# Hybrid decoder layer on one core: convolution ends in the input projection, its layer norm goes through memory in the first merge branch, operands are split in twos, PSUM is reused by bank

## Chip, cores and metric

The kernel runs on one core of one Trainium2 chip. The metric is the device time of one execution in microseconds. TensorE (PE) multiplies, with weights loaded beside it (PEld); VectorE (DVE) and ScalarE (ACT) work element by element; GpSimd (POOL) and SyncE (SP) here mostly issue DMAs. SBUF is the working memory of 128 partitions, PSUM holds matmul results in eight banks.

## The reference, cut to what matters

One layer of width 1024 on 1024 tokens, followed by an RMS norm. All is float32.

```python
h = rms_norm(x, norm_g); z = h @ w_in              # 11 blocks of 1024 columns
u = gelu(z_u); v = layer_norm(gelu(z_v))
br_a = gmlp_spatial_gate(u, v, w_s, b_s) * silu(z_ga)        # mixes tokens within chunks of 128
glu = z_ba * sigmoid(z_bb)
c = causal_depthwise_conv(glu, conv_w, conv_b)               # 31 taps along the tokens
br_b = silu(layer_norm(c, conv_ln_g, conv_ln_b)) * silu(z_gb)
br_c = cross_attention(z_q, mem_n, w_kv) * silu(z_gc)        # 4 heads, 256 memory tokens
merged = sum(sigmoid(z_m[n]) * (br[n] @ w_branch[n]) for n in (a, b, c))
out = rms_norm(x + merged @ w_out, final_norm_g)
```

## The kernel before, in words

Every float32 operand is split into a high half in the 32-bit matmul type and a low half (`split`, lines 73 to 75: ACT casts, DVE subtracts), and a product is three matmuls: high by high, high by low, low by high. Results lie with channels on partitions and tokens along the free axis.

The stages, in order of time:

1. 0 to 55 us: keys and values of the memory tokens are projected and stored (lines 195 to 369).
2. 55 to 155: block V of the input projection, its gelu and norm (lines 384 to 439); token norms, and the sums of input blocks that stage 3 needs.
3. 155 to 922: the other ten blocks of the input projection, in 40 *pairs*. `pair` (456) computes 256 output channels for all tokens from two raw weight tiles `r0`, `r1` with seven products of half size instead of eight, a scheme of sums: `s1 = a21 + a22`, `s2 = s1 − a11`, `s3 = a11 − a21`, `s4 = a12 − s2`, and ready-made input combinations T1 to T4. A product (`prod`, 444) is 12 matmuls of 128x512. The results x, z, y are PSUM banks, put together in `ca`, `cb`; the last two products of a pair and its consumer (`fin1`, `fin2`) are done during the next pair. There are four blocks of ten pairs (696 to 731), one per two tiles of 128 channels: convolution gate BB, convolution value BA, U, gate GA, GC, GB, Q, and three merge gates. GA's consumer `ugate` does the token mixing: 32 more matmuls (line 630) and DVE work.
   Beside it runs the convolution: `conv` (546) is a generator of 31 steps for one tile of 128 channels, the first on ACT, 30 on DVE (line 553). BA's consumer puts two generators in a list; `pump` advances the list by the quota `PUMP[i]` of pair i, spread over seven `fill` calls; the last two pairs have a quota of 2. A finished tile is stored in memory (`cdram`) and added into `csum` by a DMA. The sums of weights for later (`wsums`) advance by `spump`.
4. 922 to 1065: branch a is projected and gated by `merge(0, d)`, d = 0 to 7 (768 to 789, matmuls on line 778, gate on 788), the steps of attention between (`events`, 866). After each d, eight more convolution steps.
5. 1065 to 1153: branch c, `merge(2, d)`. In it the layer norm of the convolution: mean by a matmul with ones, `center` (916: subtract, square, add up), `conv_rstd`, `normed` (920: scale, silu, multiply by the gate). The eight tiles stay in SBUF as `cm`.
6. 1153 to 1306: branch b and the output projection, again with seven products each (`oprod`, 974); then the residual, the last norm, and the stores.

The program lists the work in Python order; the library that builds it arranges each engine's instructions by that order and by when they are ready, and an engine executes them one after another. Loads go by SP's queue, stores and some loads (keys, values, `cm`, `sgb`) by POOL's. A buffer is a slot of a pool: 39 slots of 4 KB per partition for most tiles, 6 for operands (`op`), 4 for half sums (`sum`), 4 for evacuated halves (`half`), 3 for raw weights. PSUM is one pool of 8 single banks up to line 759, then one of 4 double banks (line 760).

Of the kernel before, what the change touches and what calls it, by code (L numbers as in the profile page):

```python
# [39 lines left out]
def trunk(ctx, tc, xt, x, memt, wf, wv, wkf, wkv, mem, wbr, wb1, wo, wst, bs, cols, fng, out):  # L40
# [23 lines left out]
    def half(s="u"):  # L64
        return wpool.tile([P, H], F32, tag="half", name=nm(s), bufs=NHALF)
# [21 lines left out]
    def wchunk(src, raw=None):  # L87
        hi, lo = op((P, 1024), "whi"), op((P, 1024), "wlo")
        split(raw_load(src) if raw is None else raw, hi, lo)
        return hi, lo  # L90
# [48 lines left out]

    def sumsq(src, acc_tile, first, w):  # L140
        if first:
            A.activation(out=acc_tile, in_=src, func=AF.Square)
        else:
            sq = slot(shape=(P, w), s="sq")
            A.activation(out=sq, in_=src, func=AF.Square)
            V.tensor_tensor(acc_tile, acc_tile, sq, ALU.add)
# [112 lines left out]
    for g in range(2):  # L259
        pst = [bank() for _ in range(4)]  # L260
        for j in range(4):
            i = 4 * g + j
            if i == 0:
                hi, lo = op((P, 1024), "whi"), op((P, 1024), "wlo")
# [4 lines left out]
            elif g:  # L269
                hi, lo = wchunk(None, kraw[i])  # L270
            else:
                hi, lo = op((P, 1024), "whi"), op((P, 1024), "wlo")
# [171 lines left out]
    def prod(ps, w, m, start, stop):  # L444
        for k in range(4):
            ks = slice(k * P, (k + 1) * P)
            for j, (a, b) in enumerate(((0, 0), (0, 1), (1, 0))):
                T.matmul(ps, w[:, a, ks], m[k][:, b, :], start=(start and k == 0 and j == 0),  # L448
                         stop=(stop and k == 3 and j == 2), skip_group_check=not start)

    def operand(src):
        o = op()
        split(src, o[:, 0, :], o[:, 1, :])
        return o

    def pair(blk, p, consume, fill=lambda: None, last=False):
        r0, r1 = raw_load(wf[blk, 2 * p]), raw_load(wf[blk, 2 * p + 1])
        a11, a12, a21, a22 = r0[:, :H], r0[:, H:], r1[:, :H], r1[:, H:]
        s1, s2, s3, s4 = [wpool.tile([P, H], F32, tag="sum", name=nm("sum"), bufs=NSUM) for _ in range(4)]
# [13 lines left out]
        def second():  # L473
            o12 = operand(a12)
# [5 lines left out]
        V.tensor_tensor(s4, a12, s2, ALU.subtract)  # L480
# [5 lines left out]
        os2 = operand(s2)  # L486
# [4 lines left out]
        os1 = operand(s1)  # L491
# [3 lines left out]
        os3 = operand(s3)  # L495
# [7 lines left out]
        o22 = operand(a22)  # L503
        os4 = operand(s4)
# [191 lines left out]
    for p in range(4):  # L696
        for i, (blk, fn, then) in enumerate((
# [10 lines left out]
        )):  # L708
            if p == 3 and i == 8:
                for e in range(NPRE):  # L710
                    bra[e] = load(udram[e], s="bra")
            if i == 2:
                spatial_load(p)
            if i >= SP0:
                spump(1)
            share = iter(range(NFILL))

            def fill():
                k = next(share)
                n = PUMP[i] if 10 * p + i < 38 else 2  # L720
                pump(n * (k + 1) // NFILL - n * k // NFILL)

            if (p, i) == (3, 9):
                for e in range(NPRE):
                    branch_tile(e, bra[e])
            pair(blk, p, kept(fn, then), fill, (p, i) == (3, 9))
            if i == 3:
                for g in range(2 * p, 2 * p + NVA):
                    vas[g] = va_load(g)
            if i >= SP0:  # L730
                spump(SPUMP)
# [28 lines left out]
    psum = ctx.enter_context(tc.tile_pool(name="psum", bufs=4, space=PSUM))  # L760
# [40 lines left out]
    def att_q(n):  # L801
# [3 lines left out]
        qh, ql = slot(F32R, (P, 2, H), "qh"), slot(F32R, (P, 2, H), "ql")  # L805
        for d in range(2):
            qf = wpool.tile([P, H], F32, tag="sum", name=nm("qf"), bufs=NSUM)
# [70 lines left out]
    for e in range(NPRE, KT):  # L878
        branch_tile(e, load(udram[e], s="bra"))
        if e == EQ:  # L880
            att_q(0)
    merged = [None] * KT
# [5 lines left out]
    csr = wchunk(None, csum)  # L888

    def tokmean(v):  # L890
        ps = acc()
        for hf in range(2):
            for j in range(2):
                T.matmul(ps[:, hf, :], onesd, v[j][:, hf * H:(hf + 1) * H], start=(j == 0), stop=(j == 1))
        return ps
# [10 lines left out]
    cm = []  # L906
    csq = crb = crs = None

    def conv_rstd():
        nonlocal crs  # L910
        ps = misc()
        for i in range(TT):
            T.matmul(ps[:, i:i + 1], csq[:, i * P:(i + 1) * P], ones[:, 0:1], start=True, stop=True)
        crs = diagonals(mean_rsqrt(ps[:, :TT], TT, LN_EPS), TT)

    def center(e):
        V.tensor_tensor(cm[e], cm[e], csum, ALU.subtract)
        sumsq(cm[e], csq, e == 0, S)

    def normed(e):  # L920
        V.scalar_tensor_tensor(out=cm[e], in0=cm[e], scalar=c1(COL_CLG, e), in1=crb, op0=ALU.mult, op1=ALU.mult)
        A.activation(out=cm[e], in_=cm[e], func=AF.Silu, bias=c1(COL_CLB, e))
        sg = load(sgbdram[e], s="sgb", eng=G)
        V.tensor_tensor(cm[e], cm[e], sg, ALU.mult)

    for d in range(KT):
        g = merge(2, d, conv_rstd if d == 4 else None, 2)
        V.tensor_tensor(merged[d], merged[d], g, ALU.add)
        if d == 0:
            cm = [load(cdram[e], s="cm", eng=G) for e in range(KT)]  # L930
# [244 lines left out]
NFETCH = 3  # L1175
NSLOT = 39
NRAW = 3
NOP = 6
NSUM = 4
NHALF = 4  # L1180
PUMPA = 8
# [61 lines left out]
```

## Time and profile before

| | us |
|---|---|
| median of 3 runs | 1317.36 (1316.32 to 1318.34) |
| the profiled execution | 1315.63 |
| its span, first to last instruction | 1313.9 |

| engine | busy us | share of the span |
|---|---|---|
| PE | 1301.2 | 99% |
| PEld | 1085.8 | 83% |
| DVE | 1088.4 | 83% |
| ACT | 616.9 | 47% |
| POOL | 115.5 | 9% |

Busy time is the union of an engine's instructions; matmuls overlap, so PE's share says that something was always in flight, not how fast. DMA moved 249.74 MB, 190 GB/s on the mean.

### The profile page before, as it was taken

To read this page: it belongs to the slowest core of one execution; us is meant where nothing else is said; L and a number is where in the kernel's file an instruction comes from. 1 tells how busy PE (TensorE), PEld (TensorE's weight loads), DVE (VectorE), ACT (ScalarE), POOL (GpSimd) and SP (SyncE) were. 2 spreads that over 40 slices of the span, in tenths; PEclk is the share of its full clock that TensorE was granted. 3 is DMA by queue.
4 is the path that set the end of the run, shared out by engine and by line. 5 is a ranking of instruction groups with operands and counts; after the bars stand their busy time and mean duration, and the time that the engine had idled before them with its cause. 6 is when DMAs were issued, how large, how long until landed. Compare 5 with 4: busy or idle time off the path is not lost.

```text
span 1313.9 us, 16329 instructions
## 1 busy us (share of the span) xinstructions
PE 1301.2 (99%) x6010; PEld 1085.8 (83%) x6010; DVE 1088.4 (83%) x1468; ACT 616.9 (47%) x1012; POOL 115.5 (9%) x194
## 2 busy tenths in 40 slices
PE   9999999999999999999999999999999999999997
PEld 8788888888888888888888888888888888888886
DVE  6889669989959989976998996896589478895886
ACT  7667644445344445444444434445544443443245
POOL 0100000211000212001111101001000010000000
PEclk9999999999999999999999999999999999999999
DMA  9944324787425777325778436447553654655933
GB/s 340 411 158 153 136 81 132 223 270 219 139 82 161 216 225 239 130 80 166 231 232 244 129 94 158 170 172 255 194 198 123 207 194 144 224 193 220 406 126 128
DMA packets 82016, 249.74 MB, mean 190 GB/s; under 512 B 8336, under 2 KB 18064, under 8 KB 81936
## 3 DMA queue, kind: packets, MB, share of 16 engines
q1 hardware_dynamic: 55552, 153.44, 33.4%
q0 software_dynamic: 26096, 94.91, 23.2%
q8 instruction: 47, 0.77, 0.2%
q10 hardware_dynamic: 288, 0.35, 0.1%
q14 instruction: 33, 0.27, 0.1%
HBM read 176.84 MB, written 68.16 MB: 186 GB/s over the span
## 4 chain that ended last, share of the span: by engine, by line
PE 92%; DMA 4%; ACT 1%; DVE 1%; issue 1%; SPq 0%; POOL 0%; ACTq 0%; POOLq 0%
PE x L448 33%; PE y L448 17%; PE acc L778 12%; PE acc L979 10%; PE z L448 8%; PE b L402 7%; PE acc L819 2%; PE acc L855 1%; DMA raw<-in_wv 1%; PE sp L630 1%; DMA kvraw<-in_wkv 1%; DMA k<-kd 1%; PE acc L840 0%; ACT y L1124 0%; DMA mtok<-in_mem 0%
## 5 line engine op out<-in xcount | busy, mean ns | idle before, releaser
L448 PE MATMUL x<-T,op 128*128 128x512 f32 x1440 | 347.4, 390 | 0.0
L448 PEld LDWEIGHTS x<-T,op 128*128 128x128 f32 x1440 | 270.0, 188 | 56.3 <-ACT u L489 0.5
L74 ACT CAST op<-sum 128x512 fp32r<-128x512 f32 x160 | 99.4, 622 | 122.2 <-PE z L448 57.8
L553 DVE SCALAR_TENSOR_TENSOR conv<-cb,col,conv 128x994 f32<-128x994 f32 (+14 forms) x120 | 151.9, 1266 | 1.3 <-ACT conv L549 0.5
L75 DVE TENSOR_TENSOR op<-sum,op 128x512 fp32r<-128x512 f32 x160 | 109.6, 685 | 24.8 <-ACT op L74 24.6
L448 PE MATMUL x<-B,op 128*128 128x512 f32 x480 | 115.5, 389 | 0.0
L448 PE MATMUL z<-B,op 128*128 128x512 f32 x480 | 115.3, 389 | 0.0
L448 PE MATMUL y<-T,op 128*128 128x512 f32 x480 | 115.3, 389 | 0.0
L448 PE MATMUL y<-B,op 128*128 128x512 f32 x480 | 115.3, 389 | 0.0
L553 DVE SCALAR_TENSOR_TENSOR conv<-ca,col,conv 128x994 f32<-128x994 f32 (+14 forms) x90 | 113.7, 1264 | 0.4
L74 ACT CAST op<-raw 128x512 fp32r<-128x512 f32 x120 | 74.3, 620 | 73.2 <-PE y L448 71.8
L448 PEld LDWEIGHTS z<-B,op 128*128 128x128 f32 x480 | 90.1, 188 | 18.7
L448 PEld LDWEIGHTS y<-T,op 128*128 128x128 f32 x480 | 90.1, 188 | 18.7
L448 PEld LDWEIGHTS y<-B,op 128*128 128x128 f32 x480 | 90.1, 188 | 18.7
L448 PEld LDWEIGHTS x<-B,op 128*128 128x128 f32 x480 | 90.1, 188 | 18.7
L75 DVE TENSOR_TENSOR op<-raw,op 128x512 fp32r<-128x512 f32 x120 | 82.2, 686 | 24.4 <-ACT op L74 24.1
L778 PE MATMUL acc<-bhi,whi 128*128 128x512 f32 x256 | 79.7, 393 | 0.9 <-DVE ca L511 0.9
L778 PE MATMUL acc<-bhi,wlo 128*128 128x512 f32 x256 | 79.2, 390 | 0.0
L778 PE MATMUL acc<-blo,whi 128*128 128x512 f32 x256 | 79.2, 390 | 0.0
L979 PE MATMUL acc<-q,sw 128*128 128x512 f32 x288 | 65.4, 389 | 0.0
L979 PEld LDWEIGHTS acc<-q,sw 128*128 128x128 f32 x288 | 54.1, 188 | 11.2
L498 ACT COPY u<-x 128x512 f32<-128x512 f32 x40 | 23.6, 589 | 81.6 <-PE x L448 81.6
(267 smaller groups left out, 2162.1 us busy)
## 6 DMA issues: line engine op xcount, KB each, us to landing
raw<-in_wf SPq DMA_DIRECT2D x80, 512.0 KB, 3.6
sw<-sw SPq DMA_DIRECT2D x40, 512.0 KB, 7.8
sw<-wsh POOLq DMA_DIRECT2D x20, 512.0 KB, 4.3
sw<-ws POOLq DMA_DIRECT2D x20, 512.0 KB, 3.9
raw<-in_wv SPq DMA_DIRECT2D x16, 512.0 KB, 4.0
raw<-in_wbr SPq DMA_DIRECT2D x16, 512.0 KB, 5.5
gate<-g SPq DMA_DIRECT2D x16, 512.0 KB, 4.4
ws<-in_wb POOLq DMA_DIRECT2D x14, 512.0 KB, 6.4
```

The source lines that it names most:

```text
L74: A.copy(hi, src)
L75: V.tensor_tensor(lo, src, f(hi), ALU.subtract)
L402: T.matmul(pst[t], q[:, a, ts_], w[:, ws], start=(k == 0 and j == 0), stop=(k == KT - 1 and j == 2))
L448: T.matmul(ps, w[:, a, ks], m[k][:, b, :], start=(start and k == 0 and j == 0), stop=(stop and k == 3 and j == 2), skip_group_check=not start)
L498: A.copy(u3, x)
L553: V.scalar_tensor_tensor(out=a[:, PAD - j:], in0=g[:, :n], scalar=col[:, cw + j:cw + j + 1], in1=a[:, PAD - j:], op0=ALU.mult, op1=ALU.add)
L630: T.matmul(ps[:, t * P:(t + 1) * P], va[:, 4 * hf + t, :], ws[:, i, :], start=True, stop=True)
L778: T.matmul(ps[:, hf, :], w[:, ks], m[k][:, hf * H:(hf + 1) * H], start=(k == 0 and j == 0), stop=(k == KT - 1 and j == 2))
L819: T.matmul(ps[:, i, :], q[a][:, d, i * P:(i + 1) * P], kk[:, b, d, :], start=(d == 0 and j == 0), stop=(d == 1 and j == 2))
L855: T.matmul(ps[:, d, :], vv[:, a, m, d * P:(d + 1) * P], p2[b][:, m, :], start=(m == 0 and j == 0), stop=(m == MT - 1 and j == 2))
L979: T.matmul(ps[t], a[k][i][:, ts_], w[k][n], start=(start and k == 0 and j == 0), stop=(k == 3 and j == 2), skip_group_check=not start)
```

## The change

- `op` makes one tile of twice the size, for a high and a low half of 1024 columns; there are 3 of them for 6. A pair splits `r0` whole (a11, a12), then `s2` and `s1`, which lie side by side, then `r1` whole, in which `s4` has taken the place of `a21`. `s3` is split by itself into a `sum` tile. `sum` tiles are twice as wide, 2 for 4. Weight chunks, final operands and the like use the same tiles.
- The 40 pairs have an explicit order: BB and BA of the second and third block come before the last pair of the block before, those of the fourth before the last two. The quotas `PUMP` rise by one nearly throughout, from 55 to 66 per ten pairs, and hold for the last two pairs too.
- In the first merge branch no convolution steps are planned; after d = 0 what is left is done, after d = 1 the mean, after d = 2 to 4 three centrings each, after 5 the deviation, after 6 two, after 7 three of the scalings. Tiles come from memory and go back: centred ones to `ccdram`, finished ones to `brbdram`. Three scalings follow in branch c, then the quarters of the finished tiles are loaded for the last stage.
- The PSUM pool of the merges gets `reuse_waits="tile"`: a tile waits for what used its own banks, not for the whole pool before.
- Four attention units, not two, are stored in memory and loaded again (`NSPILL`).

```diff
-    def op(shape=(P, 2, H), s="op"):
-        return wpool.tile(list(shape), F32R, tag="op", name=nm(s), bufs=NOP)
+    def op(s="op"):
+        return wpool.tile([P, 2, 2 * H], F32R, tag="op", name=nm(s), bufs=NOP)
+    def wide(dt=F32, s="sum"):
+        return wpool.tile([P, 2 * H], dt, tag="sum", name=nm(s), bufs=NSUM)
...
-    def operand(src):
+    def operands(src):
         o = op()
         split(src, o[:, 0, :], o[:, 1, :])
-        return o
+        return [(o[:, 0, v], o[:, 1, v]) for v in (slice(0, H), slice(H, 2 * H))]
 
     def pair(blk, p, consume, fill=lambda: None, last=False):
...
+        s12, s3 = wide(), half("s3")
+        s2, s1 = halves(s12)
         V.tensor_tensor(s1, a21, a22, ALU.add)
         V.tensor_tensor(s2, s1, a11, ALU.subtract)
-        o11 = operand(a11)
+        o11, o12 = operands(r0)
...
         V.tensor_tensor(s3, a11, a21, ALU.subtract)
-        V.tensor_tensor(s4, a12, s2, ALU.subtract)
+        V.tensor_tensor(a21, a12, s2, ALU.subtract)
...
-        os2 = operand(s2)
+        os2, os1 = operands(s12)
...
-        os3 = operand(s3)
+        os3 = halves(wide(F32R, "os3"))
+        split(s3, *os3)
...
-        o22 = operand(a22)
-        os4 = operand(s4)
+        os4, o22 = operands(r1)
...
+    pairs = [(p, i) for p in range(4) for i in range(10)]
+    for p, back in ((1, 1), (2, 1), (3, 2)):
+        at = pairs.index((p, 0))
+        pairs[at - back:at + 2] = [(p, 0), (p, 1)] + pairs[at - back:at]
+    for p, i in pairs:
...
-                n = PUMP[i] if 10 * p + i < 38 else 2
+            n = PUMP[i]
...
-    psum = ctx.enter_context(tc.tile_pool(name="psum", bufs=4, space=PSUM))
+    psum = ctx.enter_context(tc.tile_pool(name="psum", bufs=4, space=PSUM, reuse_waits="tile"))
...
+    def center(e):
+        t = cst.pop(e)
+        center_load(e + 2)
+        V.tensor_tensor(t, t, csum, ALU.subtract)
+        store(ccdram[e], t)
+        if e == 0:
+            cst["q"] = slot(s="csq")
+        sumsq(t, cst["q"], e == 0, S)
...
+    def normed_load(e):
+        if e < KT:
+            cst[e] = load(ccdram[e], s="cn", eng=G), load(sgbdram[e], s="sgb", eng=G)
+    def normed(e):
+        t, sg = cst.pop(e)
+        normed_load(e + 2)
+        V.scalar_tensor_tensor(out=t, in0=t, scalar=c1(COL_CLG, e), in1=cst["r"], op0=ALU.mult, op1=ALU.mult)
+        A.activation(out=t, in_=t, func=AF.Silu, bias=c1(COL_CLB, e))
+        V.tensor_tensor(t, t, sg, ALU.mult)
+        store(brbdram[e], t)
     for d in range(KT):
         merged[d] = merge(0, d, lambda: events(2 * d))
         events(2 * d + 1)
-        pump(PUMPA)
-    pump(10 ** 6)
+        if d == 0:
+            pump(10 ** 6)
+        elif d == 1:
+            conv_mean()
+            center_load(0)
+            center_load(1)
+        elif d < 5:
+            for e in range(3 * d - 6, min(3 * d - 3, KT)):
+                center(e)
+        elif d == 5:
+            conv_rstd()
+            normed_load(0)
+            normed_load(1)
+        elif d == 6:
+            conv_spread()
+            for e in range(2):
+                normed(e)
+        else:
+            for e in range(2, 5):
+                normed(e)
...
+    def quadrant(src, r, c):
+        o = []
+        for j in range(2):
+            t = slot(shape=(P, 2, H), s="quad")
+            for i in range(2):
+                nc.sync.dma_start(out=t[:, i, :], in_=src[4 * r + 2 * j + i][:, c * H:(c + 1) * H])
+                o.append(t[:, i, :])
+        return o
     for d in range(KT):
-        g = merge(2, d, conv_rstd if d == 4 else None, 2)
+        g = merge(2, d, None)
         V.tensor_tensor(merged[d], merged[d], g, ALU.add)
...
+        if d < 3:
+            normed(5 + d)
+        elif d in (4, 5):
+            quads[d - 4, 0] = quadrant(brbdram, d - 4, 0)
+        elif d > 5:
+            quads[d - 6, 1] = quadrant(brbdram, d - 6, 1)
...
-NSPILL = 2
+NSPILL = 4
...
-NOP = 6
-NSUM = 4
+NOP = 3
+NSUM = 2
...
-PUMP = (6, 4, 6, 3, 6, 8, 6, 6, 5, 7)
+PUMP = (7, 5, 7, 4, 7, 8, 7, 7, 6, 8)
```

## Rows read from the trace of the kernel before

**Rows 1.** The page, busy microseconds, share of the span and instructions of each engine.

```profile
PE 1301.2 (99%) x6010; PEld 1085.8 (83%) x6010; DVE 1088.4 (83%) x1468; ACT 616.9 (47%) x1012; POOL 115.5 (9%) x194
```

**Rows 2.** By stage: start:end length, busy (instructions) per engine, clock, DMA share, GB/s.

```profile
0.00:55.00 55.00, 51.81 (x312) 46.04 (x313) 38.97 (x67) 39.37 (x65) 4.19 (x13) 1.00 0.96 371
...
155.00:922.00 767.00, 766.09 (x3444) 636.39 (x3443) 660.96 (x835) 344.91 (x541) 89.75 (x142) 1.00 0.57 177
922.00:1065.00 143.00, 142.47 (x748) 121.85 (x749) 101.97 (x102) 64.38 (x147) 10.63 (x19) 1.00 0.51 172
...
1306.00:1314.00 8.00, 0.00 (x0) 0.00 (x0) 3.50 (x13) 1.93 (x5) 0.00 (x0) 0.71 0.50 193
```

**Rows 3.** The chain in order of time: start, length, what; first and last of 38.

```profile
173.17 8.16 PE x L448 x36
...
893.89 8.16 PE x L448 x36
```

**Rows 4.** Waits of PE: us in total, times, longest.

```profile
PE acc L778 <- DVE ca L511: 0.9, 1, 0.9
...
PE acc L819 <- DMA k<-kd: 0.5, 1, 0.5
```

**Rows 5.** Timeline of PE around 920: start, length, instructions [idle before, what ended it].

```profile
918.21 2.88 PE L448 MATMUL y<-B,op 128*128 128x512 f32 x12
921.97 0.70 PE L778 MATMUL acc<-bhi,whi 128*128 128x512 f32 x2 [0.88 <-DVE ca L511]
```

**Rows 6.** Stretches of the projection by engine; the last row is line 553 alone.

```profile
349.00:406.00 57.00, 57.00 (x253) 47.19 (x252) 38.48 (x53) 25.11 (x40) 3.41 (x5) 1.00 0.37 111
...
562.00:623.00 61.00, 61.00 (x287) 51.12 (x286) 39.70 (x57) 26.79 (x41) 4.76 (x7) 1.00 0.47 130
623.00:699.00 76.00, 76.00 (x337) 62.94 (x336) 75.96 (x94) 34.49 (x55) 12.99 (x23) 1.00 0.73 231
...
775.00:836.00 61.00, 61.00 (x287) 51.12 (x286) 41.42 (x60) 27.85 (x43) 7.13 (x11) 1.00 0.59 164
...
922.00:1065.00 143.00, 37.88 (x30) 1.00 0.51 172
```

**Rows 7.** Instructions by line and shape: count, busy, mean ns, idle before.

```profile
L75 DVE TENSOR_TENSOR op<-raw,op 128x512 fp32r<-128x512 f32 x120 | 82.2, 686 | 24.4 <-ACT op L74 24.1
...
L74 ACT CAST op<-raw 128x512 fp32r<-128x512 f32 x120 | 74.3, 620 | 73.2 <-PE y L448 71.8 <-issue 1.3
...
L75 DVE TENSOR_TENSOR wlo<-raw,whi 128x1024 fp32r<-128x1024 f32 x32 | 38.9, 1219 | 14.0 <-ACT whi L74 9.8 <-PE y L448 4.1
...
L74 ACT CAST whi<-raw 128x1024 fp32r<-128x1024 f32 x32 | 33.6, 1054 | 48.1 <-PE acc L778 30.8 <-DMA raw<-in_wv 7.0 <-PE b L402 3.6
```

**Rows 8.** Timeline of DVE, then ACT: the fifth convolution tile's input, and first step.

```profile
576.99 1.22 DVE L583 TENSOR_TENSOR ca<-ca,ca 128x1024 f32<-128x1024 f32 x1
...
616.07 1.24 ACT L549 ACTIVATE conv<-ca,col 128x1024 f32<-128x1024 f32 x1
```

**Rows 9.** Timelines of DVE and PE: first operand's low half, its product; two pairs.

```profile
362.89 0.69 DVE L75 TENSOR_TENSOR op<-raw,op 128x512 fp32r<-128x512 f32 x1
...
370.19 2.88 PE L448 MATMUL x<-B,op 128*128 128x512 f32 x12
...
643.54 0.68 DVE L75 TENSOR_TENSOR op<-raw,op 128x512 fp32r<-128x512 f32 x1
...
644.87 2.88 PE L448 MATMUL x<-B,op 128*128 128x512 f32 x12
```

**Rows 10.** Timelines of POOL and PE: the last key load and the product after it.

```profile
1018.03 0.54 POOL L149 DMA_DIRECT2D cd<-conv  x1 [37.47 <-issue]
...
1019.13 0.90 POOL L153 DMA_DIRECT2D k<-kd  x1
...
1028.97 0.36 PE L819 MATMUL acc<-k,qh 128*128 128x256 f32 x1 [0.47 <-DMA k<-kd]
```

**Rows 11.** Table loads of ACT in the projection, by line.

```profile
L520 ACT ACT_TABLE_LOAD x13 | 16.7, 1283 | 0.2
```

More of the change, by code (lines that the diff above doesn't have):

```diff
@@ L87, in wchunk @@
     def wchunk(src, raw=None):
-        hi, lo = op((P, 1024), "whi"), op((P, 1024), "wlo")
-        split(raw_load(src) if raw is None else raw, hi, lo)
-        return hi, lo
+        o = op("w")
+        split(raw_load(src) if raw is None else raw, o[:, 0, :], o[:, 1, :])
+        return o[:, 0, :], o[:, 1, :]
     def flat(ps):
@@ L695, in trunk, with kinds @@
     sig, silu, gelu = apply(AF.Sigmoid), apply(AF.Silu), apply(AF.Gelu_apprx_tanh)
-    for p in range(4):
-        for i, (blk, fn, then) in enumerate((
+    def kinds(p):
+        return (
             (BLK_BB, sig, hold("b")),
@@ L707, in trunk, with fill @@
             (BLK_M0 + 1, sig, to_dram(gdram[1])(p)),
[L708 to L719, printed above, removed]
-                n = PUMP[i] if 10 * p + i < 38 else 2
[L721 to L731, printed above, removed]
+        )
+    pairs = [(p, i) for p in range(4) for i in range(10)]
[3 more added lines that the diff above has]
+    for p, i in pairs:
+        blk, fn, then = kinds(p)[i]
+        if (p, i) == (3, 8):
+            for e in range(NPRE):
+                bra[e] = load(udram[e], s="bra")
+        if i == 2:
+            spatial_load(p)
+        if i >= SP0:
+            spump(1)
+        share = iter(range(NFILL))
+        def fill():
+            k = next(share)
+            n = PUMP[i]
+            pump(n * (k + 1) // NFILL - n * k // NFILL)
+        if (p, i) == (3, 9):
+            for e in range(NPRE):
+                branch_tile(e, bra[e])
+        pair(blk, p, kept(fn, then), fill, (p, i) == (3, 9))
+        if i == 3:
+            for g in range(2 * p, 2 * p + NVA):
+                vas[g] = va_load(g)
+        if i >= SP0:
+            spump(SPUMP)
     spump(10 ** 6)
@@ L885, in trunk @@
         events(2 * d + 1)
-        pump(PUMPA)
-    pump(10 ** 6)
[L888 to L895, printed above, removed]
+        if d == 0:
[15 more added lines that the diff above has]
+                normed(e)
+        else:
+            for e in range(2, 5):
+                normed(e)
     for e in range(KT):
@@ L945, in swload @@
         for j in range(2):
-            hl = [op((P, 1024), "sw") if tag else slot(F32R, s="sw") for _ in range(2)]
+            if tag:
+                o = op("sw")
+                hl = [o[:, 0, :], o[:, 1, :]]
+            else:
+                hl = [slot(F32R, s="sw") for _ in range(2)]
             b = (SUMB, SUMO)[w][i]
@@ L966, in top, with tops @@
         return q[:, 0, :], q[:, 1, :]
-    def top2(v):
-        hi = wpool.tile([P, H], F32R, tag="sum", name=nm("bhi"), bufs=NSUM)
-        lo = wpool.tile([P, H], F32R, tag="half", name=nm("blo"), bufs=NHALF)
-        split(v, hi, lo)
-        return hi, lo
+    def tops(vs):
+        r = []
+        for v, hi in zip(vs, wides(4, F32R, "bhi")):
+            lo = half("blo", F32R)
+            split(v, hi, lo)
+            r.append((hi, lo))
+        return r
     def oprod(ps, a, w, start):
@@ L1053, in trunk, with gops @@
     gf = merged
-    def gop(v):
-        o = op()
-        split(v, o[:, 0, :], o[:, 1, :])
-        return o[:, 0, :], o[:, 1, :]
-    def gop2(v):
-        hi = wpool.tile([P, H], F32R, tag="sum", name=nm("ahi"), bufs=NSUM)
-        lo = wpool.tile([P, H], F32R, tag="half", name=nm("alo"), bufs=NHALF)
-        split(v, hi, lo)
-        return hi, lo
+    def gops(vs):
+        r = []
+        for v0, v1 in (vs[:2], vs[2:]):
+            o = op()
+            for v, q in ((v0, slice(0, H)), (v1, slice(H, 2 * H))):
+                split(v, o[:, 0, q], o[:, 1, q])
+                r.append((o[:, 0, q], o[:, 1, q]))
+        return r
     def quad(r, c):
@@ L1141, in trunk @@
     oprod(py, o, w, True)
[L1142 removed]
+    o, w = gops(s2), wn
     sums4(a21, a11, a21)
```

107 lines of the change are left out of this document (51 added, 56 removed).

## The prediction

> **What bounds the kernel now.** I read the page's busy times first, then the table by stage, then the order of the chain of work, then who TensorE waits for. TensorE is busy for 1301.2 of 1313.9 us [rows 1]. By stage [rows 2] its idle time is 3.19 us in the first 55 us (55 − 51.81), 8.00 us after the last matmul, and so 12.8 − 11.2 = 1.6 us in the 1251 us between. A busy share alone proves little, because matmuls overlap; the pace does. The chain holds 38 stretches of 36 matmuls on line 448, and each takes 8.16 us [rows 3], 227 ns from one to the next, whatever the other engines do meanwhile. The granted clock there is 1.00 of 2.4 GHz [rows 2]. So the time is the number of matmuls times a fixed pace, plus the few waits of TensorE. The longest two in the middle are 0.9 us for a DVE add and 0.5 us for a DMA [rows 4]. DVE, 661 us busy in the 767 us of the projection [rows 2], is second, not the bound.
>
> What follows for any change without fewer matmuls: it can win back at most what TensorE waits, and it can lose without limit by making TensorE wait.
>
> **The change part by part.** The sum is made against the profiled execution: 1315.63 us, span 1313.9. It lies 1.73 us below the median of 1317.36, so I add the difference found there to the median.
>
> *PSUM reused by bank.* The last projection matmuls begin at 918.21 and run 2.7 us; the first merge matmul begins at 921.97 after 0.88 us of idle, ended by the DVE add of line 511 [rows 5]. That add empties the y bank of the last pair, and the whole pool of banks had to be empty before the new pool's first tile could be written. Twelve matmuls at 227 ns from 918.21 end at 920.93, so the gap is 921.97 − 920.93 = 1.04 us. With waits by tile the first accumulator takes two of eight banks; the last pair leaves x and y busy, and other banks are free. Gain between 0 (it lands on a bank in use) and 1.04; I take 1.04, because six of the eight banks were emptied earlier.
>
> *Convolution finished in the projection.* 210 of its 240 steps already run there and 30 run in the first merge branch, 37.88 us at 1.26 each [rows 6]. There is room: DVE has three holes in the projection (57 − 38.48 = 18.5, 61 − 39.70 = 21.3, 61 − 41.42 = 19.6 us) [rows 6], 59 us in all against 38. The holes are there because the convolution work runs out: the two tiles of a block of ten pairs last until about its end, and the next two come only when pairs 0 and 1 of the next block are done. In the third block the product that feeds the convolution is ready at 578.2 (576.99 + 1.22), yet its first step starts at 616.07 [rows 8], as older steps stood ahead of it in the order and its tile came late. The diff moves those two pairs ahead by one, one and two pairs, so the holes fill from the front, and raises the quota from 55 to 66 steps per ten pairs, so that 62 steps per block leave no backlog. The order by hand: DVE takes conversion and convolution steps in program order, TensorE's order of products is otherwise kept. Cost on the path: 0, covered by DVE's idle 106 us (767 − 661); what it costs without that cover is the first rival.
>
> *Operands split two at a time.* Of seven 512-column splits in a pair, six become three 1024-column ones. On DVE one wide split is 1219 ns against 2 × 686 [rows 7], at most 0.15 × 3 × 40 = 18 us less work. But the first operand is ready later: by 1054 − 620 on ACT and 1219 − 686 on DVE [rows 7], 0.97 us. Of the seven operands the first, from raw, has least lead. Its low half ends at 363.58 for a product that begins at 370.19, a lead of 6.6 us; in the worst pair it ends at 644.22 for 644.87, 0.65 us [rows 9]. Buffers stay equal (three double tiles for six single), so the usual lead becomes about 5.6 us. The low half is first read by the third matmul, 0.45 us after the product's start. Cost 0 in the usual pair; in the worst, 0.65 + 0.45 − 0.97 = 0.1 us is left. I take 0.
>
> *Layer norm streamed in the first branch.* Eight centrings, squares and sums, and five of eight scalings, leave the second branch for the first; the centred tiles and the finished tiles go to memory and back. On DVE the first branch loses 37.88 us of steps and gains 8 × 1.22 + 7 × 1.22 + 5 × (1.28 + 1.22), some 31 us, in 143 us that were 102 busy [rows 2]; durations as for one 1024-column operation [rows 7] and the convolution steps [rows 6]. ACT gains 8 + 5 wide operations of about 1.05 us [rows 7] and two or three table loads of 1.28 [rows 11], 17 us on 64 of 143. Both fit. Memory traffic grows by 16 tiles of 0.52 MB out, 16 back and, with two more spilled attention units, about 2 MB more: 19 MB. The first branch moved 172 GB/s for 143 us, 24.6 MB; with all 19 MB in it that is 305 GB/s, and the start of this kernel moved 371 [rows 2]. TensorE gets the same matmuls earlier. On the queues: POOL's receives 8 stores of centred tiles, 5 of finished ones, 4 of attention units and some 22 loads, and the key and value loads stand in that same queue. Before, POOL waited for a convolution store until 1018.03, the key load behind it issued at 1019.13, and TensorE stood 0.47 us until 1028.97 [rows 10]. The change takes that store away but puts stores of centred tiles in its place, which also wait for DVE. Bounds: a gain of 0.5, a loss of several us (second rival); I take 0. SyncE's queue gets 16 loads of quarter tiles behind the normed stores, three merges after those; 0.
>
> *Head and tail.* The weight splits use the same bytes of buffers; the last add, scaling and store are unchanged. 0.
>
> Sum: 1315.63 − 1.04 = 1314.6 on the profiled run, 1317.36 − 1.04 = 1316.3 as a median.
>
> **The rivals.**
> *DVE late for the first operand (slower).* In the pair after GA, DVE has the gate work besides, and the quotas of these two pairs rise from 3 to 4 and from 6 to 7. Two more steps ahead of that operand's low half cost 2 × 1.26, with the wide split 2.5 + 0.97 = 3.5 us. Where what is left is 0.65 + 0.45 as in the worst pair [rows 9], TensorE waits 2.4 us; it decides where that falls under 3.5. Four blocks have such a pair: in two, 4.8 us and 1321; in all, 9.6 and 1326. For it: DVE was 75.96 of 76 us busy around the worst pair [rows 6]. Against: that was catching up a start 38 us late, which the new order avoids.
> *Key loads behind streaming stores (slower).* If one or two of the later key loads wait behind a trio of centrings, 3 × (1.22 + 1.22) = 7.3 us, TensorE has merges to do for part of it; 3 to 7 us net, 1318 to 1323, middle 1320.5. For: 0.47 us was lost that way already [rows 10]. Against: POOL then waited 37 us and TensorE only 0.47.
> *It doesn't do what it says.* The first accumulator takes the banks of the last pair, nothing else on the path moves: 1317.4.
> *A faster pace (faster).* At 2.4 GHz 512 columns take 213.3 ns, and the rows show 227. If the matmuls of the merges (768 on line 778 and 96 of the attention) ran closer together once DVE has less to read and write beside them, 864 × 13.4 ns = 11.6 us could go: 1304.7. Against: the 8.16 us are the same in the holes of DVE and where it is full [rows 3, 6]. The Trainium skill ("TensorE: Matmul & The Clock Gate", section "Wait — 56ns, not 53.3ns?") gives 215.7 ns for back-to-back matmuls of 512 columns on the full clock; by that figure 9.8 us could go. The trace does not agree: no stretch of line 448 shows it.
>
> **How the numbers follow.** Forecast 0.58 at 1316.3, with 1.5 us either side for small waits gained or lost; DVE late 0.14; key loads 0.15; no effect 0.08; faster pace, or waits in the head gone as well, 0.05. A measurement tells about 0.2%, 2.6 us, from no change. The forecast and no effect are "same" nearly whole (0.64 of 0.66, the rest split), and about 0.06 of the slow rivals stay under 2.6 us: same 0.70, slower 0.29 − 0.06 + 0.01 = 0.24, faster 0.06. The range leaves out the faster case and the worst of the slow ones: 1313.8 to 1323.
>
> **What would show it.** Right: TensorE's wait for line 511 gone, 36 matmuls still in 8.16 us, no convolution step after the projection, DVE's holes filled, and no new wait of TensorE over 1 us. Wrong by the first rival: TensorE waits at line 448 for a low half, in the pair after GA. Wrong by the second: a wait at line 819 or in the merges for a DMA, with POOL's key load just after a store. What would upset all of it is a change in matmul pace or clock.

## The result, and the profile after

The changed kernel takes 1350.26 us (median of 4 runs, 1348.87 to 1353.42), the kernel before 1316.84 beside it: 1.0258 times as long, 95% interval 1.0234 to 1.0282. Forecast was 1316.3, with a range to 1323.0. The profiled execution of the changed kernel took 1348.87 us, its span is 1346.8.

The page, busy times; then the table by stage, with the columns of [rows 2], the last line from the kernel before:

```profile
PE 1310.0 (97%) x6010; PEld 1089.8 (81%) x6010; DVE 1076.2 (80%) x1346; ACT 607.0 (45%) x891; POOL 129.3 (10%) x222
...
155.00:922.00 767.00, 764.43 (x3429) 632.94 (x3428) 682.29 (x748) 333.31 (x421) 89.70 (x143) 1.00 0.57 174
922.00:1065.00 143.00, 136.34 (x710) 116.17 (x709) 83.96 (x95) 75.59 (x161) 21.48 (x40) 0.98 0.65 240
1065.00:1153.00 88.00, 71.54 (x307) 58.40 (x306) 50.05 (x49) 26.60 (x31) 8.55 (x16) 0.88 0.75 282
...
1065.00:1153.00 88.00, 88.00 (x397) 72.77 (x396) 74.52 (x80) 40.78 (x50) 5.39 (x10) 1.00 0.53 190
```

TensorE does the same 6010 matmuls, and DVE is less busy than before (1076 us for 1088 [rows 1]). The stages of the merges show it: in 1065 to 1153, where TensorE was busy for all 88 us before, it is busy for 71.5, and the mean granted clock is 0.88 for 1.00. The waits of TensorE, in the form of [rows 4]:

```profile
PE acc L787 <- ACT bhi L83: 16.5, 1, 16.5
PE acc L902 <- ACT csh L83: 4.3, 1, 4.3
PE x L451 <- ACT u L492: 2.5, 3, 1.4
PE acc L829 <- DVE ql L84: 1.8, 1, 1.8
```

The first three are waits for ScalarE, an engine that is busy 45% of the time. To see all that TensorE loses, a slower clock too, I take the times from the start of each matmul to the start of the next, and of each that is over 330 ns what it has beyond the usual 227 ns. Summed by stretch, in us, from the records of the profiled executions:

```
                    head    projection   merges a, c   rest
                    0-156   156-927      927-1120      1120-
before              3.56    1.80         0.74          0.00
changed             3.17    5.18         29.08         0.11
```

That is 31.4 of the 32.9 us by which the spans differ, nearly all of it in the merges. The 29.08 us lie in three places: 19.7 at the boundary of branches a and c (16.6 of wait, 3.1 of half clock after it), 6.9 at the mean of the convolution (4.5 and 2.4), 2.5 between 1050 and 1062.

**The boundary.** Timeline of TensorE, then of ScalarE and VectorE, of the changed kernel:

```profile
1079.14 0.39 PE L865 MATMUL acc<-phi,v 128*128 128x512 f32 x1
1095.99 1.65 PE L787 MATMUL acc<-bhi,w 128*128 128x512 f32 x3 [16.46 <-ACT bhi L83]
...
1086.88 1.15 ACT L945 ACTIVATE cn<-cn,col 128x1024 f32<-128x1024 f32 x1 [8.98 <-DVE cn L944]
1091.48 1.15 ACT L945 ACTIVATE cn<-cn,col 128x1024 f32<-128x1024 f32 x1 [3.45 <-DVE cn L944]
1093.86 1.15 ACT L945 ACTIVATE cn<-cn,col 128x1024 f32<-128x1024 f32 x1 [1.23 <-DVE cn L944]
1094.91 3.87 ACT L83 CAST bhi<-brc 128x1024 fp32r<-128x1024 f32 x4
...
1085.57 1.28 DVE L944 SCALAR_TENSOR_TENSOR cn<-cn,col,crb 128x1024 f32<-128x1024 f32 x1 [7.49 <-DMA cn<-cc]
1092.54 1.28 DVE L944 SCALAR_TENSOR_TENSOR cn<-cn,col,crb 128x1024 f32<-128x1024 f32 x1 [1.09 <-DMA cn<-cc]
```

Read it from the bottom. DVE waits 7.49 us for a centred tile that comes back from memory; ACT's Silu step (945) waits for DVE; the casts of branch c's operands (`bhi`) stand behind three such steps, and TensorE stands behind the casts. None of the three steps is urgent: their tiles are read in branch b. Counted over the kernel, seven of the eight Silu steps run ahead of those casts; the program puts only five of them there, and the order that the library made of it has two more ahead.

Why the tile is late: POOL's and SyncE's timelines, and the load in the chain of work.

```profile
1071.93 0.53 POOL L150 DMA_DIRECT2D brb<-cn  x1 [0.30 <-DVE cn L946]
1072.46 0.54 POOL L154 DMA_DIRECT2D cn<-cc  x1
...
1070.28 4.17 SPq L154 DMA_DIRECT2D brc<-brc  x4
...
1072.46 13.08 DMA cn<-cc
```

The load of the tile that DVE waits for was issued at 1072.46, behind stores that wait for DVE themselves, and took 13.08 us to land; the DMA engines were 0.99 busy from 1080 to 1095.9. (An earlier load on POOL had stood 26.67 us for a free slot, but its tile landed at 1064.94, and DVE did not wait for it.) The four tiles of attention (`brc`) that branch c needs were asked for at 1070 to 1074 and landed at 1077.86, 1081.79, 1084.27 and 1086.82: the first before TensorE's last matmul at 1079.14, the last 8.1 us before the casts begin. So the casts did not wait for their own tiles.

**The mean.** ScalarE and TensorE of the changed kernel:

```profile
957.99 1.71 ACT L842 ACTIVATE ex<-ex,rc 128x256 f32<-128x256 f32 x4
959.59 0.61 ACT L83 CAST qh<-qf 128x512 fp32r<-128x512 f32 x1
960.10 1.05 ACT L83 CAST csh<-csum 128x1024 fp32r<-128x1024 f32 x1
...
961.21 0.50 PE L902 MATMUL acc<-csh,onesd 128*128 128x512 f32 x1 [4.33 <-ACT csh L83]
```

The last part of the sum `csum` was issued at 901.8 and landed at 906.8, some 50 us before TensorE waits. Its cast stands behind a softmax on ACT.

**The projection.** An example of the third line of TensorE's waits (line 451 for `u`); DVE, ACT, TensorE:

```profile
541.15 0.69 DVE L464 TENSOR_TENSOR sum<-raw 128x512 f32<-128x512 f32 x1 [5.35 <-DMA raw<-in_wf]
...
544.81 1.06 ACT L520 ACTIVATE ca<-ca 128x1024 f32<-128x1024 f32 x1 [4.20 <-DVE ca L513]
545.77 0.57 ACT L492 COPY u<-x 128x512 f32<-128x512 f32 x1
...
546.39 1.43 PE L451 MATMUL x<-T,os 128*128 128x512 f32 x5 [1.43 <-ACT u L492]
```

The product with `s3`, the third that a pair sums in bank x (the *third product* below), must wait until `u2` has been copied out of that bank. The copy stands on ACT behind the gate step `ca` of the pair before, that behind the add of line 513 on DVE, and that behind the first sum of the next pair, for which DVE waited 5.35 us for a raw tile.

**What came out as forecast.** The wait at the transition is gone:

```profile
922.75 2.88 PE L451 MATMUL y<-B,op 128*128 128x512 f32 x12
925.47 0.62 PE L787 MATMUL acc<-bhi,w 128*128 128x512 f32 x2
```

No idle stands ahead of the first merge matmul, for 0.88 us in [rows 5]. Line 555 (553 before) has all its 240 steps in the projection; in the three holes of [rows 6] DVE is now busy for 48.22, 60.58 and 55.27 us for 38.48, 39.70 and 41.42.

### The profile page after: what moved, and what is told of

Read it like the earlier page. It is cut to its first block, busy times and chain, and to the rows that moved or that the text cites. A ratio compares the mean times of both kernels' runs of the same rounds, so it can differ in the third digit from the quotient of the medians.

```text
span 1346.8 us, 16158 instructions
## 1 busy us (share of the span) xinstructions
PE 1310.0 (97%) x6010; PEld 1089.8 (81%) x6010; DVE 1076.2 (80%) x1346; ACT 607.0 (45%) x891; POOL 129.3 (10%) x222
## 4 chain that ended last, share of the span: by engine, by line
PE 83%; DVE 7%; DMA 5%; issue 2%; ACT 2%; POOL 0%; SPq 0%; DVEq 0%; ACTq 0%; POOLq 0%
PE x L451 28%; PE y L451 13%; PE acc L787 12%; PE acc L1047 10%; PE z L451 7%; PE b L405 6%; DVE conv L555 3%; DMA raw<-in_wf 2%; PE acc L829 2%; PE b L353 1%; PE sp L632 1%; PE acc L865 1%; DMA cn<-cc 1%; DVE op L84 1%; DMA kvraw<-in_wkv 1%
## 5 line engine op out<-in xcount | busy, mean ns | idle before, releaser
L451 PE MATMUL x<-T,op 128*128 128x512 f32 x960 | 231.9, 390 | 0.0
L451 PEld LDWEIGHTS x<-T,op 128*128 128x128 f32 x960 | 179.9, 188 | 37.2
L787 PE MATMUL acc<-bhi,w 128*128 128x512 f32 x512 | 143.4, 397 | 16.5 <-ACT bhi L83 16.5
L83 ACT CAST op<-raw 128x1024 fp32r<-128x1024 f32 x80 | 84.3, 1054 | 126.4 <-PE z L451 62.0
L787 PEld LDWEIGHTS acc<-bhi,w 128*128 128x128 f32 x512 | 97.2, 192 | 37.4 <-ACT bhi L83 16.9
L451 PE MATMUL x<-T,os 128*128 128x512 f32 x480 | 116.2, 391 | 2.6 <-ACT u L492 2.5
L451 PEld LDWEIGHTS x<-T,os 128*128 128x128 f32 x480 | 89.5, 188 | 23.5 <-ACT u L492 5.1
L84 DVE TENSOR_TENSOR op<-raw,op 128x1024 fp32r<-128x1024 f32 x80 | 97.3, 1218 | 0.7 <-ACT op L83 0.6
L787 PE MATMUL acc<-blo,w 128*128 128x512 f32 x256 | 80.5, 396 | 0.0
L83 ACT CAST op<-sum 128x1024 fp32r<-128x1024 f32 x40 | 42.2, 1055 | 73.4 <-PE y L451 41.2
```

Of the source, the lines that this page charges most:

```text
L83: A.copy(hi, src)
L84: V.tensor_tensor(lo, src, f(hi), ALU.subtract)
L451: T.matmul(ps, w[a][:, ks], m[k][:, b, :], start=(start and k == 0 and j == 0), stop=(stop and k == 3 and j == 2), skip_group_check=not start)
L787: T.matmul(ps[:, hf, :], w[:, ks], m[k][:, hf * H:(hf + 1) * H], start=(k == 0 and j == 0), stop=(k == KT - 1 and j == 2))
```

## The experiments

Theory A says that in-order engines are the cause: steps of no hurry, waiting for tiles that come from memory, stand ahead of casts that TensorE needs. Its rivals: the tiles that TensorE needs are late themselves, for memory traffic and slots (B); the loss only moves to branch b (C); the wide splits or the new order of pairs cost a large part (D). Each run has its own runs of the kernel before beside it: 1316.55 us for the first four runs, 1316.04 for the next four, 1316.48 for the last four. All sums of excess below are made as in the table above.

**Splits of branch c ahead of the scalings.**

```diff
-        else:
-            for e in range(2, 5):
-                normed(e)
 
     for e in range(KT):
...
                 split(unit[2 * (e // 2) + tb][:, e % 2, :], bhi[e][:, hs], blo[e][:, hs])
+    for e in range(2, 5):
+        normed(e)
```

> The changed kernel with one move: the operand splits of branch c stand in the program ahead of the three scalings normed(2), normed(3), normed(4) of the last merge of branch a, not behind them. Theory A (head of line): ACT and DVE execute in order, and the casts of bhi stood behind three Silu steps that waited for cn tiles loaded back from memory; TensorE's 16.6 us at the boundary of branches a and c then fall to what the brc loads themselves leave. Those were issued at 1070.3 to 1074.4 and land some 11 us later, 1081 to 1085, against 1079.1 when TensorE runs out: 2 to 6 us are left, with less half-clock time after it. Total about 1335, 1331 to 1339. Rival B (memory and slots): the tiles of branch c are late by themselves, for the slots and the traffic; the wait stays over 12 us, total 1346 to 1350. Rival C: the wait goes but comes back where branch b reads its quarters, as the scalings end later; total over 1342 with a new wait on line 1047.

1330.28 us, 1.0113 times before (1.0097 to 1.013): 20.0 us of the 33.4 are gone by the order of a few steps. TensorE and ScalarE at the boundary now:

```profile
1080.57 1.42 PE L787 MATMUL acc<-bhi,w 128*128 128x512 f32 x5 [0.35 <-ACT bhi L83]
...
1079.47 1.05 ACT L83 CAST bhi<-brc 128x1024 fp32r<-128x1024 f32 x1 [0.88 <-DMA brc<-brc]
1082.12 1.06 ACT L83 CAST bhi<-brc 128x1024 fp32r<-128x1024 f32 x1 [1.60 <-DMA brc<-brc]
```

The tiles do come one by one, 2.5 us apart, but TensorE takes them at that pace, and 0.35 us of wait are left: less than the 2 to 6 that I had set. B falls for the boundary: the four tiles landed as late as in the changed kernel (1079.45 to 1086.97), and the wait is gone. C falls: the rest after 1120 has 0.51 us of excess.

**Sum of the convolution split earlier.**

```diff
+    def conv_split():
+        cst["m"] = slot(F32R, s="csh"), slot(F32R, s="csl")
+        split(csum, *cst["m"])
+
     def conv_mean():
-        v = slot(F32R, s="csh"), slot(F32R, s="csl")
-        split(csum, *v)
+        v = cst.pop("m")
...
             pump(10 ** 6)
+            conv_split()
```

> The changed kernel with one move: csum is split (ACT cast, DVE subtract) right after the convolution has ended, ahead of the second merge, not after the attention steps that follow it; the mean's matmuls stay where they were. Theory A: csum was complete long before (its last add into it was issued at 901.8), and its cast stood on ACT behind a softmax that waited for DVE; TensorE's 4.3 us and the half-clock matmuls after it go, together 6.9 us over 956.5 to 965.6: total 1343.4, 1341.5 to 1345.5. Rival: csum itself is late, or another operand is waited for at the same place: the wait stays, total 1349 to 1351.

1340.98 us (1.0197, 1.0179 to 1.0214): 9.3 us less than the changed kernel, for 6.9 expected, and 0.5 us under the range. The profiled executions differ by 8.6 us (1348.87 and 1340.24), and the excess in the merges by 7.4 (29.08 and 21.69). The wait for `csh` is gone, and the one at the boundary is 15.6 us for 16.5; `csum` had been there.

**Both.** The two edits above, in one kernel.

> Both moves together. Theory A: the gains add up, 15 + 7 us: about 1328, 1324 to 1333, still some 10 us above the kernel before, made of 3.9 us of waits for u2 in the projection, 2.5 us around 1050 to 1060, and what is left at the boundary. Rival B or C: 1340 or more.

1323.37 us (1.0055, 1.0039 to 1.0072), 0.6 us under the 1324 to 1333 expected. The gains nearly add up: 26.9 us for 20.0 and 9.3 apart. The excess is 4.93 us in the projection and 4.51 in the merges. The waits of TensorE in the merges that are left:

```profile
PE acc L829 <- DVE ql L84: 1.8, 1, 1.8
PE acc L865 <- DVE plo L84: 1.3, 1, 1.3
...
PE acc L787 <- DVE sgc L867: 0.8, 1, 0.8
```

For one of them the cause can be read: the split that makes `plo` begins on DVE at 1008.96, behind three centrings (3.49 us from 1004.41) and an add to the sum of squares (1.22 us). For the other two it was not followed up.

**The layer norm as before, all else changed.** The functions of the streamed layer norm are taken out, `cm`, `csq` and `normed` of the kernel before put back into branch c, and two attention units are spilled.

```diff
-    ccdram, brbdram = spills("cc"), spills("brb")
...
-            conv_mean()
-            center_load(0)
-            center_load(1)
...
+    csr = wchunk(None, csum)
...
+        for e in range(3 * d, min(3 * d + 3, KT)):
+            center(e)
...
+        if d >= 4:
+            normed(2 * d - 8)
+            normed(2 * d - 7)
...
-NSPILL = 4
+NSPILL = 2
```

> The changed kernel with the layer norm as it was before: mean, centring and scaling in branch c, its eight tiles kept on chip, two spilled attention units, no tiles through memory. Convolution finished in the projection, splits in twos and PSUM by bank stay. Theory A: all that is lost in the merges is the streamed layer norm; what stays is the projection, with 3.9 us of excess at third products that wait for the copy u2, less 1.04 us at 921 and some tenths at the key load: 1319.5, 1317.5 to 1321.5. Rival D (the wide splits or the new order of pairs cost a large part, also in the merges): 1328 or more. Rival E (the projection's waits come from the streaming too): 1315 to 1317.

1320.47 us (1.0032, 1.0018 to 1.0045). The merges have 0.11 us of excess, the projection 5.81. So streaming the layer norm, with the two further spilled units, costs 1350.26 − 1320.47 = 29.8 us, all of it in the merges (a run below takes the two units out again, and the excess in the merges stays), and D holds for some 4 us in the projection: four waits of third products, 3.6 us in all.

**Order of pairs and PSUM alone, single splits.** The kernel before with the list of pairs, the quotas `PUMP` and `reuse_waits="tile"`; what is left of the convolution is done after d = 0.

```diff
-    for p in range(4):
-        for i, (blk, fn, then) in enumerate((
...
+    pairs = [(p, i) for p in range(4) for i in range(10)]
+    for p, back in ((1, 1), (2, 1), (3, 2)):
...
-        pump(PUMPA)
-    pump(10 ** 6)
+        if d == 0:
+            pump(10 ** 6)
...
-PUMP = (6, 4, 6, 3, 6, 8, 6, 6, 5, 7)
+PUMP = (7, 5, 7, 4, 7, 8, 7, 7, 6, 8)
```

> The kernel before with two parts of the change alone: the new order and quotas of the pairs with the convolution finished in the projection, and PSUM by bank. Splits stay single (512 columns), the layer norm stays in branch c. It differs from the run with the old layer norm only in the splits and their tiles. Theory S (the wide splits cost the projection's 4 to 5 us): TensorE's excess at third products goes, 1.04 us at line 921 and the key load's 0.64 stay gained: 1315, 1313.5 to 1316.5. Theory O (the order of pairs and the higher quotas cost it): 1319 to 1321, with the waits for u2 as before.

1317.76 us (1.0018, 1.0009 to 1.0027): between the two. The four waits are gone, so they need the wide splits; whether wide splits with the old order of pairs have them too was not run. But one of 2.64 us is new:

```profile
664.60 1.65 PE L448 MATMUL x<-T,op 128*128 128x512 f32 x6 [2.64 <-ACT u L489]
...
663.02 1.06 ACT L518 ACTIVATE ca<-ca 128x1024 f32<-128x1024 f32 x1 [5.84 <-DVE ca L511]
663.98 0.57 ACT L489 COPY u<-x 128x512 f32<-128x512 f32 x1
...
661.13 1.25 DVE L553 SCALAR_TENSOR_TENSOR conv<-cb,col,conv 128x998 f32<-128x998 f32 x1
662.30 0.69 DVE L511 TENSOR_TENSOR ca<-y,u 128x512 f32<-128x512 f32 x1
```

It is the same copy, `u2`, behind the same gate step; here DVE is late because it does convolution steps between all else, three pairs after GA.

**Five halves for four.**

```diff
-NHALF = 4
+NHALF = 5
-NSLOT = 39
+NSLOT = 38
```

> The run with the old layer norm again, with five evacuation halves for four (and 38 slots for 39 to make room). Since s3 became a half, four are taken per pair of a ring of four, so that u2 of a pair takes the place of u2 of the pair before, which is free only when line 513 has read it; before, three were taken of four. Theory H (this ring makes u2 late): the waits at third products go, 1316, 1314.5 to 1317.5. Theory R (the raw tiles make it late): no change, 1319.5 to 1321.5.

1331.98 us (1.0125, 1.011 to 1.0141): neither. The profiled execution is the shortest of its four, 1327.94 us. In it the waits for `u2` stay (3.9 us in four), so the ring of halves is not what holds it. New ones come: 2.8 us for a cast at 240.9 and 2.4 us for the tiles `va` (line 632), and with them the transition's wait for line 513 is back (0.8 us). They came with the slot that was taken away, or with the half that was given; the run alone does not tell which.

**Four raw tiles for three.**

```diff
-NRAW = 3
+NRAW = 4
-NSLOT = 39
+NSLOT = 38
```

> The run with the old layer norm again, with four raw weight tiles for three (and 38 slots for 39). Theory R: a raw tile lands late (541.1, after DVE had been idle for 5.35 us at line 464), and DVE, in order, does the two sums and the wide split of the next pair ahead of the add on line 513, so that ACT's gate step and u2 behind it come late; with a fourth tile the load is issued earlier, the waits at third products go: 1316, 1314.5 to 1317.5. Theory H: no change, 1319.5 to 1321.5. If both this and the run with five halves keep the waits, it is DVE's order with wide splits itself.

1319.85 us (1.0031, 1.002 to 1.0041). The time is that of theory H; the trace is not. The four waits of third products are gone, as theory R has it, and the slot is not what took them away, as the run with five halves gave up the same slot and kept waits for `u2`. The time is not won. The slot that was given for it brings 2.0 us of waits for `va` at line 632 and 0.8 at the transition, much as in the run before, and a wait of 2.7 us for `u2` comes up at 645.3, two pairs after GA. There DVE stood 5.85 us for ACT's cast of `wsh`, and ACT 6.50 us for the load of `ws`, ahead of the add. That R alone explains the wide splits' loss is thus supported, not shown by the time.

**Both edits, two spilled units.** The run with both edits, and:

```diff
-NSPILL = 4
+NSPILL = 2
```

> The run with both moves (splits of branch c first, csum split early), with two attention units through memory for four, as before the change. Theory: the two further units were no cause; the waits that are left in the merges (1.6 us at 1008, 1.9 at 1047, 1.1 at 1056) come from the streamed steps on ACT and DVE and stay: 1322 to 1325. Rival: the further units cost part of them by their stores and loads on POOL's and SP's queues, or by slots: 1320 or less; or they had been needed for slots, and the wait at the boundary comes back: over 1327.

1325.59 us (1.0077, 1.0064 to 1.0091), 0.6 us over the 1322 to 1325 expected. The excess in the merges is 4.71 us for 4.51: the two further units were no cause of the waits in the merges. The 2 us more lie in the projection (7.02 for 4.93), in waits for `u2` (4.4 us for 2.9); why an edit behind the projection changes them was not followed up.

**The gate step behind the copy.** Two runs with one edit: in the run with order and PSUM alone, and in the one with the old layer norm. `keep` pins an instruction behind the one ahead of it in the program.

```diff
-        A.copy(u2, x)
+        keep(A.copy(u2, x))
+        if eat:
+            eat.pop(0)()
...
             V.tensor_tensor(ca[:, H:], y, u2, ALU.add)
-            consume(ca, cb, x)
+            eat.append(lambda: consume(ca, cb, x))
...
-            A.activation(out=ca, in_=ca, func=func)
+            keep(A.activation(out=ca, in_=ca, func=func))
```

> The run with order and PSUM alone (1317.76), with one edit: on ACT the gate step of the pair before (the activation of ca, line 518 there) is placed behind the copy u2, not ahead of it. In that run TensorE waited 2.8 us at 661.6 for u2; u2 stood on ACT behind ca, and ca waited 5.84 us for the add of line 511, which stood on DVE between convolution steps. Theory (head of line on ACT): the wait goes, 1314.9, 1313.8 to 1316. Rival: the consumer, moved later, makes something else late (PSUM banks, the convolution's input, the gate of tokens): no gain or slower, 1317 to 1320.

1315.01 us, 0.9986 times before (0.9977 to 0.9995). The wait is gone, and the projection has 0.76 us of excess, the least of all runs up to here.

> The same edit in the run with the old layer norm and splits in twos (1320.47; third products wait 1.19, 0.83, 1.44 and 0.83 us). There u2 also takes the ring place of the u2 before, which line 513 frees, so that only ACT's step ca (1.06 us) is taken out of the way: 0.13 + 0 + 0.38 + 0 us are left, and 1316.7, 1315.3 to 1318. Rival: the place in the ring and DVE's late add alone set u2; no gain, 1319.5 to 1321.5.

1330.6 us (1.0107, 1.0092 to 1.0121): 10 us slower than without the edit, where 4 less were expected. The waits for `u2` shrink to 1.1 us, but the first operand now comes late, and the excess in the projection is 14.46 us for 5.81. Waits of TensorE; then DVE and TensorE in one such pair:

```profile
PE x L451 <- DVE op L84: 8.0, 4, 3.2
...
470.38 0.69 DVE L464 TENSOR_TENSOR sum<-raw 128x512 f32<-128x512 f32 x1 [6.40 <-DMA raw<-in_wf]
472.12 1.25 DVE L557 SCALAR_TENSOR_TENSOR conv<-cb,col,conv 128x994 f32<-128x994 f32 x1
473.29 0.68 DVE L515 TENSOR_TENSOR ca<-y,u 128x512 f32<-128x512 f32 x1
473.89 0.68 DVE L465 TENSOR_TENSOR sum<-sum,raw 128x512 f32<-128x512 f32 x1
474.49 1.22 DVE L84 TENSOR_TENSOR op<-raw,op 128x1024 fp32r<-128x1024 f32 x1
...
475.76 2.56 PE L451 MATMUL x<-B,op 128*128 128x512 f32 x10 [1.64 <-DVE op L84]
```

DVE stands 6.40 us at the next pair's raw tile (51.3 us over the kernel, for 33.4 without the edit), and what follows it comes late: with `u2` out of the way, the wide split of the first operand. Why the raw tiles land later under this edit was not tried.

**PSUM by bank alone.** The kernel before, and:

```diff
-    psum = ctx.enter_context(tc.tile_pool(name="psum", bufs=4, space=PSUM))
+    psum = ctx.enter_context(tc.tile_pool(name="psum", bufs=4, space=PSUM, reuse_waits="tile"))
```

> The kernel before with PSUM reused by bank and nothing else: the one term of the sum on record. Theory: 1.04 us less, 1315.0, 1314.3 to 1315.6. Rival: the wait at 921 turns into one for the weights or the operand of the first merge, 1315.7 to 1316.5.

1315.23 us, 0.9991 (0.9982 to 1.0), beside 1316.48: 1.25 us less, for 1.04 expected. The interval only just reaches 1, and the profiled execution is no shorter than that of before (span 1314.0 for 1313.9), as its first 156 us have 4.63 us of excess for 3.56. That the wait for line 511 is gone from the trace is the surer sign.

**Fewer steps after GA.** The run with order and PSUM alone, with other quotas.

```diff
-PUMP = (7, 5, 7, 4, 7, 8, 7, 7, 6, 8)
+PUMP = (8, 6, 8, 4, 6, 7, 5, 7, 7, 8)
```

> The run with order and PSUM alone (1317.76), with the quotas of convolution steps moved to the pairs ahead of GA and the last ones: 8, 6, 8, 4, 6, 7, 5, 7, 7, 8 for 7, 5, 7, 4, 7, 8, 7, 7, 6, 8, the same 66 in ten. Theory (the higher quota after GA fills DVE, so that line 511 and with it u2 come late at 661.6): the 2.8 us go, 1314.9, 1313.8 to 1316. Rival: the steps are a backlog and come at the same place whatever the quota, or the wait moves to another pair: 1316.5 to 1320.

1314.88 us, 0.9985 (0.9976 to 0.9994). The 2.64 us are gone, with 0.76 us of excess in the projection, as in the run with the gate step behind the copy. With the run of the gate step this shows both ends of one chain: less ahead of line 511 on DVE, or `ca` out of the way on ACT, and `u2` is in time. These two are the shortest of all kernels here, though not to be told from PSUM by bank alone.

## Why the prediction was wrong

*PSUM by bank:* −1.04 us, right in place, and in size as far as the time can tell (1.25 as measured, with an interval from 0 to 2.4).

*Convolution finished in the projection:* 0 was right for the changed kernel, and the cover named, DVE's holes, did fill. (The quotas of before add up to 57 per ten pairs, not 55; the new ones to 66.) With single splits the new order and quotas cost 2.64 us at one place, gone with other quotas. It lies three pairs after GA, as the worst pair of [rows 9] does, with DVE full. But the first rival priced the first operand's low half; the wait was for a copy out of PSUM.

*Splits in twos:* taken as 0, they cost 1320.47 − 1317.76 = 2.7 us by the medians. The intervals of the two runs overlap, and the run with single splits has a wait of 2.64 us of its own; what the traces show of the wide splits is the four waits, 3.6 us. The step that failed is "Of the seven operands the first, from raw, has least lead". It looked at operands alone. In the usual pair of [rows 9] the first operand's lead is 6.6 us; just ahead of it, in the kernel before, ACT's copy `u2` and the product with `s3` are these:

```profile
364.95 0.59 ACT L489 COPY u<-x 128x512 f32<-128x512 f32 x1 [0.93 <-PE x L448]
...
367.47 2.88 PE L448 MATMUL x<-T,op 128*128 128x512 f32 x12
```

The copy ends at 365.54, a lead of 1.9 us, though nothing but the product that it copies had held it up. The wait that came out is that of the third product for `u2`, through DVE's add, ACT's gate step and the copy, 0.68 + 1.06 + 0.57 us, in the 5.4 us that two products take; no row for it stood in the prediction. DVE saved what was reckoned: 660.96 + 37.88 − 682.29 = 16.6 us for at most 18, and it was worth nothing, as DVE was not the bound. The Trainium skill ("Perfetto Trace Analysis", section "Optimizing Scalar/DVE Operations") says that where the two engines aren't saturated but cause bubbles on others, breaking up instructions may help. The runs with wide and with single splits fit it from the other side: here instructions were joined, with DVE busy for 682 of 767 us, and 2.7 us lost.

*Layer norm streamed:* taken as 0, with "a gain of 0.5, a loss of several us" as bounds; measured 29.8 us. This is the term that decided, and the step that failed in it is the one from "Both fit" to a cost of 0. It summed DVE's and ACT's new work against their idle time in the stage, and it did fit: DVE 83.96 of 143 us, ACT 75.59. What a sum of busy time cannot show is what stands behind what. The queues of POOL and SyncE were walked through, those of ACT and DVE were not, though the diff puts steps that wait for memory directly ahead of the casts of branch c and puts the cast of `csum` behind a softmax. Two of the three losses in the merges are shown by moving one part each, 20.0 and 9.3 us; what is left of the streaming is 1323.37 − 1320.47 = 2.9 us, in the waits for `ql`, `plo` and `sgc`.

*Traffic:* the forecast of up to 305 GB/s was near (240 and 282 in the two stages, for 172 in [rows 2]), and not what decided: with the first edit the bytes are the same and 20 us are gone. It had a part, as the centred tile took 13.08 us to land, but nothing that TensorE needed had to stand behind it.

*The half clock* had no term. The waits took 16.6 and 4.5 us, what followed them 3.1 and 2.4 more.

*Rivals.* Key loads: no wait of TensorE for `k` in the changed kernel. "DVE late for the first operand": seen only in the run with the gate step behind the copy, 8.0 us in four, 2.0 each on the mean for the 2.4 priced. No effect: the wait at the transition is gone. A faster pace: the stretches of 36 matmuls still take 8.16 us. No rival had the mechanism that decided, so the range ended 27 us short.

## What to carry to other kernels

On ACT and DVE each step here ran behind the one ahead of it, however long that one waited; so for every step that a change moves, list what stands behind it on its own engine, and ask who needs that, above all where the step waits for a load. A free share of busy time answers whether the work fits, never when it is done. Put what the bound engine needs next ahead of what is merely due, and look for the least lead not among operands alone but among the copies out of PSUM too.

## What the runs showed of the hardware

TensorE at half clock. After the 16.5 us of wait, and after the 4.3, the matmuls come 426 to 427 ns apart, at a granted clock of 0.50 and 0.59 (by stretch, columns as in [rows 2]; the last two lines are from the run with wide splits and the gate step behind the copy):

```profile
961.50:965.50 4.00, 3.47 (x9) 2.46 (x9) 2.35 (x3) 1.01 (x1) 1.09 (x2) 0.59 0.74 234
...
1096.00:1101.80 5.80, 5.80 (x13) 4.29 (x14) 5.80 (x7) 5.80 (x9) 1.60 (x3) 0.50 0.97 304
...
373.00:377.00 4.00, 4.00 (x11) 3.17 (x12) 4.00 (x5) 0.69 (x2) 0.00 (x0) 0.58 0.00 0
852.80:857.00 4.20, 4.18 (x18) 3.49 (x19) 4.13 (x4) 1.14 (x2) 0.53 (x1) 1.00 0.61 250
```

That is the lower level, 1.2 GHz, for some 4 to 6 us of work. In the long wait the granted clock had fallen already (0.55 from 1080 to 1095.9), in the short one it had not (1.00 from 957 to 961). It is not the length of the wait alone that decides. In the run with wide splits and the gate step behind the copy, 2.6 us from one matmul's start to the next at 370 were followed by seven matmuls at 426 to 427 ns, and 3.6 us at 849 by none; in the run with order and PSUM alone, 3.0 us at 661.6 were followed by none (clock 1.00 from 664.6 to 668). The Trainium skill ("TensorE: Matmul & The Clock Gate", section "Wait — 56ns, not 53.3ns?") gives 426.7 ns from one matmul of 512 columns to the next at the lower clock, and the trace agrees; its 215.7 ns at the upper no run here shows, the pace is 227 ns throughout.
